# Three gaps of 16 bytes in the rows that the matmuls read

## The chip, the cores and the metric

One NeuronCore of a Trainium2 chip runs the whole program. The metric is the device time of one execution in microseconds (us); the kernel before took 2957.85 us in the median of three runs (2950.77, 2957.85 and 2959.75). TensorE (PE) multiplies, and its weight loads are shown apart as PEld. VectorE is DVE, ScalarE is ACT, GpSimd is POOL and SyncE is SP.

## The reference, cut to what matters

The reference is a two-layer decoder trunk for 256 tokens of width 2048, all in float32. Layer 0 mixes with a gated DeltaNet, layer 1 with differential attention; each is followed by an MLP and a gated embedding:

```python
h = h + gated_deltanet(rmsnorm(h, norm_mix[0]), ...)      # layer 0
h = h + diff_attention(rmsnorm(h, norm_mix[1]), k, v, ...)  # layer 1
hn = rmsnorm(h, norm_mlp[i])
h = h + jnp.square(jax.nn.relu(hn @ mlp_w1[i])) @ mlp_w2[i]   # 2048 -> 8192 -> 2048
gate = jax.nn.sigmoid(rmsnorm(h, norm_ple[i]) @ ple_w_gate[i])
h = h + (p[i] @ ple_w_proj[i]) * gate
```

After layer 0 the stream is normalised once more and projected to the keys and values of layer 1. Nearly all arithmetic is the product of 256 rows with a large weight matrix.

## The kernel before, in words

Every large product is made of two halves of each operand: a value is rounded to fp32r (the "hi" half), the rest is the "lo" half, and three matmuls (hi·hi, hi·lo, lo·hi) are summed in PSUM. `chunk` (lines 118 to 134) brings 1 MB of weights with one DMA from SP's queue into `raw`, ACT rounds it 1024 columns at a time into `whi` (line 131), and DVE subtracts into `wlo` (line 132). Three buffers each let this run ahead of PE.

Two loops use the pieces. They differ in what stands still in the array:

- `g2` (lines 137 to 153) makes a transposed product. A 128x128 block of weights is the stationary operand, and the 256 columns of one k tile of x are the moving one. For each k tile and each block of 128 output columns there is a triple: line 150 (`xh` past `whi`), line 151 (`xl` past `whi`), line 152 (`xh` past `wlo`). It is used for the gates, keys, queries and values of the DeltaNet, for the first half of the MLP, and for queries and keys of the attention: 3600 triples, 10,800 matmuls of 256 columns.
- `g1` (lines 155 to 169) makes a plain product. A 128x128 block of x is stationary, and 512 columns of weights move, in triples of lines 166, 167 and 168. It is used for z of the DeltaNet, V of the attention, and every output product.

In the MLP, `first(q)` is a block of 256 triples of `g2` (768 matmuls) and `second(q)` one of `g1`; they run in the order first 0, first 1, second 0, first 2, second 1, first 3, second 2, second 3.

`xpair` (lines 200 to 203) allots one tile `xh` and one `xl` with room for 16 k tiles of 256 floats and 128 floats more, and hands out two views of each: one that begins `SHIFT` = 112 floats (448 bytes) into the tile, and one that begins at 0. Each k tile is a row of 256 floats (1024 bytes), and row follows row without a gap. The shifted view (`self.xa`, and `xb` in the attention) is the moving operand of all of `g2`; it is also the stationary operand of `g1` for z and V (384 triples). The view at 0 (`self.xs`, `oT`) is stationary only. `transposed` (lines 185 to 198) fills a view row by row: ACT writes the hi half (line 197) and DVE the lo half (line 198).

As built, the tiles `xh` and `xl` and all `raw`, `whi` and `wlo` tiles begin at multiples of 512 bytes within a partition, the hidden halves `hidh` and `hidl` (and `ph`, `pl`) 256 bytes past one, and `oh` and `ol` 384 bytes past one. So in `g2` every moving row begins 448 bytes past a multiple of 512 and every stationary block at a multiple of 512.

The float32 operands of lines 389 and 666 begin at a multiple of 512 and 32 bytes past one.

The order of the work is that of the program on each engine; PE takes its matmuls in that order.

Of the kernel before, what the change touches and what calls it, by code (L numbers as in the profile page):

```python
# [18 lines left out]
T = 256  # L19
NT = T // P  # L20
KD = D // P
# [11 lines left out]
SHIFT = 112  # L33
LAM_INIT = 0.8 - 0.6 * math.exp(-0.3 * 1)
POST = 1.0 - LAM_INIT


class Trunk:
    def __init__(self, ctx, tc, d, out):
        self.ctx, self.tc, self.nc, self.d, self.out = ctx, tc, tc.nc, d, out  # L40
        pool = lambda name, bufs, **kw: ctx.enter_context(tc.tile_pool(name=name, bufs=bufs, **kw))
        self.const = pool("const", 1)
        self.wraw = pool("wraw", 3)
        self.whl = pool("whl", 3)
        self.main = pool("main", 1)
        self.small = pool("small", 2)
        self.acc = pool("acc", 4, space=bass.MemoryType.PSUM)
        self.mis = pool("mis", 4, space=bass.MemoryType.PSUM)
        self.dram = pool("dscr", 1, space=bass.MemoryType.DRAM)
# [6 lines left out]
    def constants(self):  # L56
# [3 lines left out]
        nc.vector.memset(self.eps[:, 1:2], EPS * HD)  # L60
        nc.vector.memset(self.eps[:, 2:3], EPS / POST ** 2)
        nc.scalar.activation(self.eps[:, 3:4], self.eps[:, 0:1], AF.Sqrt)
# [137 lines left out]
    def xpair(self, pool, which):  # L200

        tiles = [pool.tile([P, KD * T + 128], F32R, name=n + which) for n in ("xh", "xl")]
        return tuple(tuple(t[:, o:o + KD * T].rearrange("p (k t) -> p k t", k=KD) for t in tiles) for o in (SHIFT, 0))

    def rowcast(self, r, dst):

# [416 lines left out]
    def attention(self, h):  # L623
        nc, tc, d = self.nc, self.tc, self.d
        with ExitStack() as c:
# [60 lines left out]
            def values(hd, aT):  # L686
# [7 lines left out]
                for t in range(NT):  # L694
                    nc.scalar.activation(o[:, t * T:(t + 1) * T], po[:, t * T:(t + 1) * T], AF.Square, accum_out=ss[:, t:t + 1])
                nc.scalar.activation(ss, ss, AF.Sqrt, scale=1.0 / (2 * HD * POST ** 2), bias=self.eps[:, 2:3])
                nc.vector.reciprocal(ss, ss)
# [95 lines left out]
```

## Time and profile before

| what | value |
|---|---|
| median of three runs | 2957.85 us |
| profiled execution | 2951.79 us, of which the span from first to last instruction is 2950.0 us |
| mean granted TensorE clock | 0.996 |
| PE busy | 2909.7 us (99% of the span), 18730 matmul records |
| DVE busy | 1782.8 us (60%) |
| ACT busy | 1451.8 us (49%) |
| DMA | 527.19 MB, mean 179 GB/s |

Matmuls overlap in the records: a matmul of 256 columns is shown with 0.28 us, while the next starts 0.11 or 0.12 us after it. So pace is read from start to start, or from how many matmuls a stretch of time holds (a count takes in those that had begun before the stretch, so one matmul's length is added to the stretch).

### The profile page before, as it was taken

What the parts mean: (1) busy time and instruction counts of PE and PEld (TensorE: products, weight loads), DVE (VectorE), ACT (ScalarE), POOL (GpSimd) and SP (SyncE); (2) the same over time, 40 slices, a digit from 0 to 9 for tenths busy, and PEclk for the clock granted to TensorE, in tenths of its full rate; (3) what the DMA queues carried; (4) which work ended last, traced back from release to release, by engine and by line L of the source; (5) the groups of instructions that cost most, each with busy time, mean ns of one, the idle gap of its engine ahead of it and who ended that gap; (6) DMA issues with size and microseconds to landing.
All of it is one profiled execution on the core that took longest, in us unless ns stands there. A gap on an engine that the chain in (4) does not pass through costs nothing.

```text
span 2950.0 us, 44777 instructions
## 1 busy us (share of the span) xinstructions
PE 2909.7 (99%) x18730; PEld 2626.2 (89%) x18730; DVE 1782.8 (60%) x2324; ACT 1451.8 (49%) x1947; POOL 60.4 (2%) x64
## 2 busy tenths in 40 slices
PE   8999999999999999999999999999999999999998
PEld 8989889988988998989988889987899899898886
DVE  7879766666666555555555565567555555555565
ACT  5655555545545443444434553367544444344454
POOL 1011000000000000000000000000000000000000
PEclk9999999999999999999999999999999999999999
DMA  6654544455445665655565556654566565556654
GB/s 200 207 168 140 175 161 138 149 175 161 133 143 182 194 196 190 188 194 189 186 198 189 178 170 198 191 166 144 183 192 197 189 192 192 188 186 198 202 172 155
DMA packets 289595, 527.19 MB, mean 179 GB/s; under 512 B 25966, under 2 KB 44560, under 8 KB 289264
## 3 DMA queue, kind: packets, MB, share of 16 engines
q1 hardware_dynamic: 288160, 521.77, 55.3%
q8 instruction: 147, 2.41, 0.3%
q0 software_dynamic: 816, 2.03, 0.2%
q10 hardware_dynamic: 416, 0.53, 0.1%
q14 instruction: 56, 0.46, 0.0%
HBM read 520.03 MB, written 4.26 MB: 178 GB/s over the span
## 4 chain that ended last, share of the span: by engine, by line
PE 93%; DVE 4%; ACT 2%; DMA 0%; issue 0%; POOL 0%; ACTq 0%; DVEq 0%
PE accb L166 16%; PE accb L167 16%; PE accb L168 16%; PE accb L151 13%; PE accb L152 13%; PE accb L150 13%; PE misb L429 2%; DVE wlo L132 1%; ACT whi L131 1%; PE misb L434 1%; PE misb L412 0%; PE misb L444 0%; PE misb L193 0%; PE misb L421 0%; DMA h<-x 0%
## 5 line engine op out<-in xcount | busy, mean ns | idle before, releaser
L132 DVE TENSOR_TENSOR wlo<-raw,whi 128x1024 fp32r<-128x1024 f32 x970 | 1190.1, 1228 | 985.0 <-ACT whi L131 983.6
L131 ACT CAST whi<-raw 128x1024 fp32r<-128x1024 f32 x970 | 1019.2, 1051 | 1296.8 <-PE accb L168 677.5
L150 PE MATMUL accb<-xha,whi 128*128 128x256 f32 x3344 | 939.4, 281 | 0.8 <-ACT whi L131 0.8
L151 PE MATMUL accb<-xla,whi 128*128 128x256 f32 x3344 | 937.6, 280 | 1.6 <-DVE xla L198 1.6
L152 PE MATMUL accb<-xha,wlo 128*128 128x256 f32 x3344 | 936.9, 280 | 0.5 <-DVE wlo L132 0.5
L152 PEld LDWEIGHTS accb<-xha,wlo 128*128 128x128 f32 x3344 | 633.2, 189 | 0.7 <-DVE wlo L132 0.7
L151 PEld LDWEIGHTS accb<-xla,whi 128*128 128x128 f32 x3344 | 629.7, 188 | 2.4 <-DVE xla L198 2.2
L150 PEld LDWEIGHTS accb<-xha,whi 128*128 128x128 f32 x3344 | 630.4, 189 | 1.4 <-ACT whi L131 1.0
L168 PE MATMUL accb<-whi,hidl 128*128 128x512 f32 x1024 | 398.5, 389 | 0.0
L167 PE MATMUL accb<-wlo,hidh 128*128 128x512 f32 x1024 | 398.5, 389 | 0.0
L166 PE MATMUL accb<-whi,hidh 128*128 128x512 f32 x1024 | 398.5, 389 | 0.0
L166 PE MATMUL accb<-whi,xha 128*128 128x512 f32 x640 | 254.2, 398 | 1.2 <-ACT xha L197 1.2
L167 PE MATMUL accb<-wlo,xha 128*128 128x512 f32 x640 | 252.8, 395 | 0.1
L168 PE MATMUL accb<-whi,xla 128*128 128x512 f32 x640 | 251.9, 394 | 0.0
L168 PEld LDWEIGHTS accb<-whi,hidl 128*128 128x128 f32 x1024 | 192.3, 188 | 40.1
L166 PEld LDWEIGHTS accb<-whi,hidh 128*128 128x128 f32 x1024 | 192.3, 188 | 39.9
L167 PEld LDWEIGHTS accb<-wlo,hidh 128*128 128x128 f32 x1024 | 192.3, 188 | 39.1
L166 PEld LDWEIGHTS accb<-whi,xha 128*128 128x128 f32 x640 | 120.4, 188 | 26.2 <-ACT xha L197 2.5
L167 PEld LDWEIGHTS accb<-wlo,xha 128*128 128x128 f32 x640 | 120.5, 188 | 25.0 <-DVE wlo L132 1.4
L168 PEld LDWEIGHTS accb<-whi,xla 128*128 128x128 f32 x640 | 120.3, 188 | 24.2
L166 PE MATMUL accb<-whi,oh 128*128 128x512 f32 x256 | 101.1, 395 | 0.8 <-ACT oh L469 0.8
L167 PE MATMUL accb<-wlo,oh 128*128 128x512 f32 x256 | 101.1, 395 | 0.0
(276 smaller groups left out, 2616.5 us busy)
## 6 DMA issues: line engine op xcount, KB each, us to landing
raw<-mlp_w SPq DMA_DIRECT2D x256, 1024.0 KB, 5.2
raw<-gdn_w_in SPq DMA_DIRECT2D x97, 1024.0 KB, 5.1
raw<-gdn_w_out SPq DMA_DIRECT2D x32, 1024.0 KB, 5.0
raw<-ple_w_gate SPq DMA_DIRECT2D x32, 1024.0 KB, 5.0
raw<-w_kv SPq DMA_DIRECT2D x32, 1024.0 KB, 5.2
raw<-diff_w_q SPq DMA_DIRECT2D x16, 1024.0 KB, 5.0
raw<-diff_w_o SPq DMA_DIRECT2D x16, 1024.0 KB, 5.0
gcb<-gcd SPq DMA_DIRECT2D x16, 256.0 KB, 4.3
```

Source lines behind the costliest of these rows:

```text
L131: nc.scalar.copy(hi, sl)
L132: nc.vector.tensor_tensor(lo, sl, hi.bitcast(F32), ALU.subtract)
L150: nc.tensor.matmul(o, hi[:, k, cs], xh[:, kt], start=kt == 0 and ct % 2 == 0, stop=False, skip_group_check=True)
L151: nc.tensor.matmul(o, hi[:, k, cs], xl[:, kt], start=False, stop=False, skip_group_check=True)
L152: nc.tensor.matmul(o, lo[:, k, cs], xh[:, kt], start=False, stop=kt == nk - 1, skip_group_check=True)
L166: nc.tensor.matmul(banks[t], xh[:, kt, ts], hi[:, k], start=kt == 0, stop=False)
L167: nc.tensor.matmul(banks[t], xh[:, kt, ts], lo[:, k], start=False, stop=False)
L168: nc.tensor.matmul(banks[t], xl[:, kt, ts], hi[:, k], start=False, stop=kt == nk - 1)
L429: nc.tensor.matmul(ps[:, h * P:(h + 1) * P], NTt[:, 2 * h + c], X[:, h * P:(h + 1) * P], start=True, stop=True)
L434: nc.tensor.matmul(ps[:, h * P:(h + 1) * P], UB[:, 2 * h + c], X[:, h * P:(h + 1) * P], start=True, stop=True)
```

## The change

The shifted view is no longer one block of 16 rows. A small class holds four blocks of four rows, and each block begins 4 floats (16 bytes) later than it would have, counted from the one before. Rows 0 to 3 stay where they were, 448 bytes into the tile; rows 4 to 7 lie 16 bytes later than before, rows 8 to 11 lie 32 bytes later, rows 12 to 15 lie 48 bytes later. The room of 128 floats at the tile's end holds it: no tile changes its size or place. The view at 0 is as it was.

```diff
+class Rows:
+    def __init__(self, tile, first):
+        n = KD // 4 * T
+        self.parts = [tile[:, first + g * (n + 4):first + g * (n + 4) + n].rearrange("p (k t) -> p k t", t=T) for g in range(4)]
+
+    def __getitem__(self, at):
+        k = at[1]
+        return self.parts[k // (KD // 4)][(at[0], k % (KD // 4)) + tuple(at[2:])]
...
     def xpair(self, pool, which):
         tiles = [pool.tile([P, KD * T + 128], F32R, name=n + which) for n in ("xh", "xl")]
-        return tuple(tuple(t[:, o:o + KD * T].rearrange("p (k t) -> p k t", k=KD) for t in tiles) for o in (SHIFT, 0))
+        return tuple(Rows(t, SHIFT) for t in tiles), tuple(t[:, :KD * T].rearrange("p (k t) -> p k t", k=KD) for t in tiles)
```

No instruction is added, removed or moved on any engine, and each waits for what it waited for. What differs are start addresses: of one operand of 8964 matmuls (8100 moving rows in `g2`, 864 stationary blocks in `g1`), of the output of 60 writes by ACT, and of the output and one input of 60 by DVE.

## Rows read from the trace of the kernel before

**Rows 1.** The page: busy time, PE clock by slices, the chain.
```profile
PE 2909.7 (99%) x18730; PEld 2626.2 (89%) x18730; DVE 1782.8 (60%) x2324; ACT 1451.8 (49%) x1947; POOL 60.4 (2%) x64
...
PEclk9999999999999999999999999999999999999999
...
PE 93%; DVE 4%; ACT 2%; DMA 0%; issue 0%; POOL 0%; ACTq 0%; DVEq 0%
```

**Rows 2.** Waits of PE, longest first: us in total, times, longest.
```profile
PE misb L193 <- DVE w_mix L76: 3.4, 1, 3.4
...
PE accb L152 <- DVE wlo L132: 1.8, 3, 0.7
PE accb L150 <- ACT xhb L197: 1.6, 2, 1.2
```

**Rows 3.** Busy time by windows of `g2`: us, busy (xcount), clock, DMA, GB/s.
```profile
56.00:76.00 20.00, 20.00 (x172) 20.00 (x171) 14.44 (x20) 10.97 (x12) 0.00 (x0) 1.00 0.69 227
28.00:51.00 23.00, 23.00 (x198) 23.00 (x197) 18.78 (x30) 12.73 (x15) 0.00 (x0) 1.00 0.56 182
91.00:159.00 68.00, 68.00 (x579) 68.00 (x579) 55.50 (x98) 37.70 (x50) 0.00 (x0) 1.00 0.67 205
932.00:1102.00 170.00, 170.00 (x1503) 170.00 (x1502) 96.10 (x99) 81.73 (x95) 0.00 (x0) 1.00 0.61 192
1190.00:1279.00 89.00, 89.00 (x758) 89.00 (x757) 46.82 (x46) 39.90 (x44) 0.00 (x0) 1.00 0.60 190
1759.00:1919.00 160.00, 160.00 (x1414) 160.00 (x1413) 80.95 (x75) 62.24 (x59) 0.00 (x0) 1.00 0.62 197
2134.00:2303.00 169.00, 169.00 (x1494) 169.00 (x1493) 95.09 (x98) 81.33 (x95) 0.00 (x0) 1.00 0.62 193
```

**Rows 4.** Instructions in order of time on PE, MLP of layer 0: start, us.
```profile
1189.69 0.39 PE L168 MATMUL accb<-whi,hidl 128*128 128x512 f32 x1
1189.92 0.28 PE L150 MATMUL accb<-xha,whi 128*128 128x256 f32 x1
1190.04 0.28 PE L151 MATMUL accb<-xla,whi 128*128 128x256 f32 x1
1190.15 0.28 PE L152 MATMUL accb<-xha,wlo 128*128 128x256 f32 x1
1190.27 0.28 PE L150 MATMUL accb<-xha,whi 128*128 128x256 f32 x1
```

**Rows 5.** Weight loads by group, 1368 to 1457 us: xcount | busy us, mean ns.
```profile
L152 PEld LDWEIGHTS accb<-xha,wlo 128*128 128x128 f32 x253 | 48.6, 192 | 0.0
L150 PEld LDWEIGHTS accb<-xha,whi 128*128 128x128 f32 x252 | 47.3, 188 | 0.0
```

**Rows 6.** Line 168 of `g1`: duration ns min/median/max, first and last start us.
```profile
L168 PE MATMUL accb<-whi,hidl x1024: 388/389/394, 1103.3 to 2833.3; 128*128 128x512 f32 x171
L168 PE MATMUL accb<-whi,ol x256: 390/393/404, 323.3 to 923.9; 128*128 128x512 f32 x128
L168 PE MATMUL accb<-whi,xlb x128: 387/389/485, 2032.5 to 2125.4; 128*128 128x512 f32 x128
```

**Rows 7.** Matmuls by group in V of the attention, 1926 to 1940 us.
```profile
L168 PE MATMUL accb<-whi,xla 128*128 128x512 f32 x21 | 8.3, 394 | 0.0
L167 PE MATMUL accb<-wlo,xha 128*128 128x512 f32 x21 | 8.2, 392 | 0.0
L166 PE MATMUL accb<-whi,xha 128*128 128x512 f32 x21 | 8.2, 388 | 0.0
```

**Rows 8.** Two float32 matmuls of 256 columns: duration ns min/median/max.
```profile
L389 PE MATMUL misb<-kT x32: 377/379/382, 187.5 to 859.1; 128*128 128x256 f32 x32
L666 PE MATMUL misb<-kT,qT x32: 379/381/383, 1942.7 to 2045.9; 128*128 128x256 f32 x32
```

**Rows 9.** Line 197, ACT's writes of the hi halves: duration ns min/median/max.
```profile
L197 ACT ACTIVATE xha<-misb,cols x80: 454/480/540, 925.2 to 2845.3; 128x256 fp32r<-128x256 f32 x80
L197 ACT ACTIVATE xha<-misb,w_mix x16: 465/473/488, 17.2 to 26.8; 128x256 fp32r<-128x256 f32 x16
```

## The prediction

> **What bounds the kernel now.** I read the page first. PE is busy for 99% of the span, the chain that ended last runs over PE for 93%, and the granted clock stands at full speed in every slice, so it is at the 2.4 GHz level throughout [rows 1]. The waits of PE come next: the longest entry is 3.4 us in total, and the one for weights just 1.8 us [rows 2]. So nothing feeds PE too late. The kernel lasts as long as PE's matmuls take one after another, and only their pace matters.
>
> A clock that stands still should mean one pace for equal matmuls. The windows say otherwise [rows 3]. In the first two MLP blocks of layer 0 (932 to 1102 us), 1503 matmuls of 256 columns fit into 170.28 us (the window and one matmul's 0.28): 113.3 ns each. In the attention (1759 to 1919) it is 160.28/1414 = 113.4, in layer 1's first two blocks 169.28/1494 = 113.3. But in the third block of layer 0 it is 89.28/758 = 117.8 ns, and in the DeltaNet's first stages 117.7, 117.6 and 117.9 (20.28/172, 23.28/198, 68.28/579). The third and fourth block of both layers, four in all, read like the row 1190:1279. Nothing waits there either: PE is busy in the whole window, the clock is the same, DMA share and GB/s are alike. I call these the fast and the slow pace; they differ by 4.5 ns.
>
> Two more things matter about them. The slow pace is there from the first matmul: the first one after a `g1` block at 1189.92, the next starts 0.12, 0.11, 0.12 us later [rows 4]. And it holds for a whole block of 768, as the fast one holds for two blocks. In the slow pace every third weight load is longer, 192 ns beside 188 [rows 5]. So the slow pace is something between the moving row's stream and the weight load that runs beside it, and once the two run at a given offset in time they keep it.
>
> Does the address decide? In `g1` the same 512 moving columns run past stationary blocks at different addresses. Past the hidden tile (256 bytes past a multiple of 512) and past the attention's `xlb` at 0 a record lasts 389 ns, past `ol` at 384 it lasts 393 [rows 6]. Past `xa` at 448, in V, the three lines last 388, 392 and 394, which is 7 ns a triple more than three times 389 [rows 7]. Taken as distance from stationary to moving start, modulo 256 bytes: 0 costs nothing, 128 about 4 ns a matmul, 192 about 2.3. In `g2` the distance is 64 (stationary at 0, moving at 448), and costs 0 or 4.5. So addresses do count, and 0 is a clean distance in `g1`.
>
> **The change, part by part.** *Instructions.* None is added or moved, so no wait, queue or DMA changes by itself. The 60 writes of ACT and 60 of DVE go to starts 16, 32 or 48 bytes later. Line 197 took 480 ns in the median for one group and 473 for another of the same shape [rows 9]; if the new starts cost that difference either way, it is 60 x 7 ns = 0.4 us. I take 0.
>
> *Moving rows of `g2`.* Three quarters of 10,800 matmuls, 8100, read from a new phase. Named stretches at the slow pace are four MLP blocks of 768 (3072) and 172 + 198 + 579 in the early DeltaNet, 4021 in all: 4021 x 4.5 ns = 18.1 us is what the slow pace costs today. Named stretches at the fast pace are four MLP blocks (3072) and the attention's 1536: 4608. The remaining 2171 are cut into short groups by the DeltaNet's small matmuls; I leave them out.
>
> The new distances are 48, 32 and 16 for the second, third and fourth quarter. No row has such a distance. The nearest are 64 (0 or 4.5 ns) and 0 (nothing, in `g1`). Read as a straight line between them, the slow share of the moved quarters falls to three quarters, a half and a quarter of today's, a half on average: 18.1 x 0.75 x 0.5 = 6.8 us gained. That reading treats each matmul by itself. The other takes into account that a pace holds: 16 k tiles come round for every 512 output columns, the last quarter at distance 16, and the first quarter of the next round follows it without a pause. If a stream that has become fast at 16 or 32 stays fast when it comes back to 64, only the first quarters after each restart stay slow, and nearly all is gained; I put it at 0.85 of 18.1 = 15.4 us. I take the middle of the two, 11 us. The ends of this term are a gain of 18.1 (all fast) and a loss of 4608 x 4.5 = 20.7 us (all that is fast becomes slow), without a cost that belongs to the phase alone, below.
>
> *Stationary blocks of `g1`.* 384 triples of `xa` at 7 ns are 2.7 us. Their distance goes from 192 to 208, 224 and 240, towards the clean 256. By the same straight line three quarters of them lose half: 2.7 x 0.75 x 0.5 = 1.0 us gained. Ends: 2.7 gained, or, at the 4 ns a matmul of distance 128, 864 x (4 - 2.3) = 1.5 us lost.
>
> *Cover.* A faster PE needs its weights sooner. In the fast windows DMA moves 192 to 197 GB/s at a share of 0.61 to 0.62 and PE stays busy throughout [rows 3], so the slow blocks can be fed at the fast pace too. In the DeltaNet's short groups part of a gain may turn into waiting for DVE; those groups are not in the sum.
>
> *Sum.* Against the profiled execution's own 2951.8 us (span 2950.0, 1.8 around it): 2951.8 - 11 - 1 = 2939.8. The median of the runs shown is 6 us higher, which is about what 1350 more matmuls at the slow pace would make, so executions may differ in which stretches are slow. I add half of it: 2943 us.
>
> **A rule against this.** Between one stationary address and another, line 168's record goes from 389 to 394 ns at one clock [rows 6, 7]. The Trainium skill, "TensorE: Matmul & The Clock Gate", section "Step-by-step: what each phase is for", says that PE reads the moving operand and the weights through two independent ports, so that loading the next weights takes no read bandwidth from the running matmul. By that rule the start address is of no account and the change makes 0 us. Rows 6 and 7 speak against it in its plain form; the same outcome is rival 1.
>
> **Rivals.**
> 1. *Start addresses do nothing here, or what is gained in one stretch is lost in another.* For it: both paces exist at one and the same distance of 64, so the address alone doesn't decide. Against it: `g1`'s four distances [rows 6, 7]. By itself 0 us, by the straight line alone 8 us gained; with the 3 us for the median that is 2947 to 2955, and the runs shown scatter up to 2960.
> 2. *The new phases hold the slow pace.* The place is the MLP's fast blocks and the attention. The rows would be no better at 16 to 48 than at 64, and a stream kicked at each quarter would fall into the slow pace and stay. Price: 4608 x 4.5 = 20.7 us, or 15.6 if only the moved three quarters are slow. It decides the sign when more than about half of the fast matmuls turn. From 2951.8 and the 3 us for the median that gives 2970 to 2976, with the short groups up to 2982. For it: the third MLP block is slow from its first matmul, though the `g1` block ahead of it ran without a pause [rows 4], so the slow pace is easily entered.
> 3. *A row that doesn't start on a 64-byte boundary touches 17 pieces of 64 bytes instead of 16.* The fast pace of 113.3 ns is 272 cycles of 2.4 GHz for 256 columns, 17 for each 16 columns, and 16 columns are 64 bytes. If every piece touched costs 17 cycles, however little of it is used, a moved row costs 289 cycles, 7.1 ns more: 8100 x 7.1 = 57 us, about 3005. If it costs one cycle for the boundary alone, 0.42 ns, it is 3.4 us. Against it: the float32 matmuls whose operands start 32 bytes past a multiple of 64 (line 666) last 381 ns, those at 0 (line 389) last 379 [rows 8]; 2 ns on 8100 rows would be 16 us. But these stream more slowly, so they bound it loosely.
>
> **How the numbers follow.** The forecast (the slow pace goes in good part, 2926 to 2949) has 0.45. Rival 1 has 0.24, rival 2 has 0.17, rival 3 in its large form 0.10, and 0.04 is left for anything else on either side. A measurement of this kernel can tell about 0.3%, here 9 us, so faster begins below 2949. Faster: 0.45 and a little of rival 1, 0.47. Slower: rivals 2 and 3 and a little of rival 1 and the rest, 0.31. The same: 0.22. The likeliest case gives 2943, its own range is 2926 to 2949. The range that should hold 8 in 10 goes from 2926, which leaves the two slow terms all gone with a little of the DeltaNet's short groups, up to 2982, the top of rival 2; rival 3 is left outside.
>
> **What would show it.** In the windows after the change, the third and fourth MLP blocks should hold about 788 matmuls in 89 us instead of 758, and weight loads of 192 ns should become rare. If the pace changes every four k tiles (48 matmuls), the address acts on each matmul by itself; if a block is of one pace throughout, the lock in time rules. V's three lines should come nearer to 389. The prediction is wrong if the blocks that were fast read 117.8 or more, if a third pace near 120 ns appears in the moved quarters (rival 3), or if the counts in all windows stand as they were.

## The result, and the profile after

The changed kernel took 2971.74 us in the median of five runs (2969.56 to 2975.82), the kernel before 2956.84 (2950.77 to 2959.75). The ratio is 1.0063, with an interval of 1.005 to 1.0077: 0.6% slower, where 0.5% faster was forecast. Ratios here and below are the recorded ones, which compare the runs of the two kernels and needn't be the quotient of the two medians (here 1.005). One execution of the last run below, 3203.12 us at a granted clock of 0.849, is left out of its ratio.

The page shows the same machine with nothing new to wait for. The first line is the busy time of each engine, the second the granted clock by slices, the others the longest wait of PE and that for weights:

```profile
PE 2929.8 (99%) x18730; PEld 2645.0 (89%) x18730; DVE 1783.2 (60%) x2324; ACT 1452.6 (49%) x1947; POOL 58.1 (2%) x64
...
PEclk9999999999999999999999999999999999999999
...
PE misb L205 <- DVE w_mix L88: 4.2, 1, 4.2
...
PE accb L164 <- DVE wlo L144: 1.6, 3, 0.7
```

PE has the same 18730 matmuls as in [rows 1], is busy 20.1 us longer, and the span grew by 20.8 us, from 2950.0 to 2970.8. The longest wait of PE grew by 0.8 us, the one for weights is 0.2 shorter [rows 2]. So the time went into the pace of the matmuls themselves. The windows of [rows 3], read in the changed kernel (us, busy and count of PE, PEld, DVE, ACT, POOL, then clock, DMA share, GB/s):

```profile
932.00:1102.00 170.00, 170.00 (x1453) 169.98 (x1452) 94.73 (x101) 81.46 (x98) 0.00 (x0) 1.00 0.58 181
1190.00:1279.00 89.00, 89.00 (x725) 87.48 (x724) 47.40 (x47) 40.02 (x44) 0.00 (x0) 1.00 0.60 188
28.00:51.00 23.00, 23.00 (x197) 23.00 (x197) 18.88 (x30) 12.30 (x15) 0.00 (x0) 1.00 0.53 172
91.00:159.00 68.00, 68.00 (x582) 68.00 (x582) 54.99 (x96) 38.31 (x50) 0.00 (x0) 1.00 0.67 207
```

The first two MLP blocks hold 1453 matmuls where they held 1503: 170.28/1453 = 117.2 ns instead of 113.3. The stretches that ran at 117.8 hardly differ: 117.3 instead of 117.9 from 91 to 159 us, 118.2 instead of 117.6 from 28 to 51, and 117.2 from 1215 to 1265 (below; the window from 1190 now begins in `g1`, whose matmuls are longer). So not one pace took over from the other; there are new ones. One round of 16 k tiles in layer 1's MLP shows them. The rows are the first matmul of each quarter of four k tiles, and of the next round (start, us):

```profile
2190.57 0.28 PE L162 MATMUL accb<-xha,whi 128*128 128x256 f32 x1
...
2196.04 0.28 PE L162 MATMUL accb<-xha,whi 128*128 128x256 f32 x1
...
2201.76 0.28 PE L162 MATMUL accb<-xha,whi 128*128 128x256 f32 x1
...
2207.44 0.28 PE L162 MATMUL accb<-xha,whi 128*128 128x256 f32 x1
...
2213.07 0.28 PE L162 MATMUL accb<-xha,whi 128*128 128x256 f32 x1
```

A quarter is 48 matmuls. It takes 5.47, 5.72, 5.68 and 5.63 us: 114.0 ns a matmul in the quarter that stayed at distance 64 (stationary start minus moving start, modulo 256 bytes), 119.2 at distance 48, 118.3 at 32, and 117.3 at 16. Over the whole program, from start to start, the means are 114.7, 119.1, 118.3 and 117.3, and every block of the MLP and the attention has the last three to 0.1 ns.

The sum closes. I add up the times from one matmul's start to the next within `g2`, and take off 113.33 ns each (226.67 in `g1`). Times over 150 ns (300 in `g1`), mostly at restarts and waits, stay out. What is left over was 22.8 us in `g2` and 7.5 in `g1`; now it is 41.7 and 9.4. That is 18.9 and 1.9 us more, 20.8 together, the whole growth of the span; with the long times it is 21.4, so what else changed is under 1 us. By quarters, `g2`'s 41.7 are 3.4 (distance 64), 14.8, 13.1 and 10.4; the 22.8 before were 6.1, 5.8, 5.6 and 5.3.

V of the attention answers to [rows 7] (xcount | busy us, mean ns):

```profile
L179 PE MATMUL accb<-wlo,xha 128*128 128x512 f32 x21 | 8.3, 394 | 0.0
L180 PE MATMUL accb<-whi,xla 128*128 128x512 f32 x21 | 8.2, 393 | 0.0
L178 PE MATMUL accb<-whi,xha 128*128 128x512 f32 x20 | 7.9, 394 | 0.0
```

The three lines last 394, 393 and 394 ns, a sum of 1181 where it was 1174: V did not come nearer to 389, it moved away. From start to start, z and V went from 229.2 and 229.3 ns a matmul to 230.5 and 231.0.

### The profile page after: what moved, and what is told of

Its sections match the earlier page's. It is cut to its first block, busy times and chain, and to the rows that moved or that the text cites. A ratio compares the mean times of both kernels' runs of the same rounds, so it can differ in the third digit from the quotient of the medians.

```text
span 2970.8 us, 44777 instructions
## 1 busy us (share of the span) xinstructions
PE 2929.8 (99%) x18730; PEld 2645.0 (89%) x18730; DVE 1783.2 (60%) x2324; ACT 1452.6 (49%) x1947; POOL 58.1 (2%) x64
## 4 chain that ended last, share of the span: by engine, by line
PE 95%; DVE 3%; ACT 1%; DMA 1%; issue 0%; POOL 0%; ACTq 0%; SPq 0%; DVEq 0%
PE accb L179 16%; PE accb L178 16%; PE accb L180 16%; PE accb L163 14%; PE accb L164 13%; PE accb L162 13%; PE misb L441 2%; DVE wlo L144 1%; PE misb L446 1%; PE misb L424 0%; ACT whi L143 0%; PE misb L456 0%; PE misb L205 0%; PE misb L433 0%; DMA raw<-gdn_w_in 0%
```

## The experiments

The pace of the kernel before in the two windows that the runs below are read in, one at either of its paces:

```profile
960.00:1080.00 120.00, 120.00 (x1061) 120.00 (x1061) 66.80 (x65) 56.86 (x64) 0.00 (x0) 1.00 0.62 194
1215.00:1265.00 50.00, 50.00 (x427) 50.00 (x426) 27.94 (x29) 23.63 (x27) 0.00 (x0) 1.00 0.59 184
```

That is 120.28/1061 = 113.4 ns and 50.28/427 = 117.8 ns. In the changed kernel:

```profile
960.00:1080.00 120.00, 120.00 (x1025) 120.00 (x1025) 65.00 (x63) 55.55 (x63) 0.00 (x0) 1.00 0.60 187
1215.00:1265.00 50.00, 50.00 (x429) 50.00 (x428) 26.41 (x27) 23.18 (x26) 0.00 (x0) 1.00 0.60 190
```

117.3 and 117.2 ns. My theory after the result was that a start off a multiple of 64 bytes costs; the question was whether it is the moving row's own start or its difference from the weights'. The runs whose edit shows `self.parts` start from the changed kernel, and so do the two scans; the others start from the kernel before.

**Is 0 a clean distance?**

```diff
-SHIFT = 112
+SHIFT = 0
```

> The shifted view begins at 0 bytes instead of 448, without gaps, so that moving row and weight block both begin at multiples of 512 bytes in g2. Theory A (what costs is the difference of moving row and weight block within 64 bytes, here 0): g2 stays at its two paces of 113.3 and 117.8 ns, no 119, and z and V lose their 7 ns a triple; total 2930 to 2957 us. Theory B (the moving row's own start within 64 bytes costs, whatever the weights do; here 0): the same. Theory C (the distance modulo 256 bytes sets a sliding price: 64 gave 113.3, 48 gave 119.1, 32 gave 118.3, 16 gave 117.3, so 0 should give about 116): all of g2 near 116 ns, no block at 113.3; about 2957 us.

```profile
960.00:1080.00 120.00, 120.00 (x1002) 120.00 (x1001) 64.48 (x63) 54.22 (x63) 0.00 (x0) 1.00 0.58 182
1215.00:1265.00 50.00, 50.00 (x419) 50.00 (x418) 26.02 (x26) 22.34 (x26) 0.00 (x0) 1.00 0.58 183
```

2993.27 us, ratio 1.0146 (1.0131 to 1.0161). Every block of the MLP and the attention runs at 120.0 ns, the slowest pace of all the longer stretches, with both operands at multiples of 512 bytes. Theories A and B, which put the price on bytes within 64, had 2957 at most and fall as they stood; so does C's straight line, which had 116. In `g1` the same distance is good: z and V came down from 229.2 and 229.3 to 227.8 and 228.6 ns. What is clean in `g1` is the worst in `g2`.

**One phase alone, without jumps.**

```diff
-SHIFT = 112
+SHIFT = 120
```

> No gaps; all rows of the shifted view begin 480 instead of 448 bytes into the tile, 32 bytes past a multiple of 64, while the weights stay where they are. All three theories: every g2 block runs at the 118.3 ns that the third quarter showed, none at 113.3. 10,800 matmuls x (118.3 - 115.5, the mean before) = 30 us more: about 2987 us. Had the loss come from the jumps between phases and not from the phases, g2 would stay at 113.3 and 117.8 and the time near 2957.

```profile
960.00:1080.00 120.00, 120.00 (x1017) 120.00 (x1016) 64.86 (x64) 55.98 (x64) 0.00 (x0) 1.00 0.59 187
1215.00:1265.00 50.00, 50.00 (x425) 50.00 (x424) 27.08 (x26) 22.38 (x26) 0.00 (x0) 1.00 0.60 189
```

2982.76 us, ratio 1.011 (1.0095 to 1.0125). 118.3 ns in both windows, as the third quarter of the changed kernel. So the distance itself costs, and not the jumps between distances.

**Own start or difference?**

```diff
+        self.pad = pool("pad", 1)
+        self.pad.tile([P, 8], F32, name="pad")
         self.whl = pool("whl", 3)
```

> The kernel before with 32 bytes of padding ahead of all weight buffers and activations, so that moving rows and weight blocks alike begin 32 bytes past a multiple of 64, at the same differences as before. Theory A and C (differences count): g2 at 113.3 and 117.8 ns, g1 past the hidden tile at 226.7, about 2957 us. Theory B (a row's own start counts): g2 at 118.3 throughout as with the weights left in place, +30 us, and g1's moving weights slower too; 2985 us or more.

```profile
960.00:1080.00 120.00, 120.00 (x1061) 120.00 (x1061) 66.43 (x64) 57.13 (x65) 0.00 (x0) 1.00 0.62 195
1215.00:1265.00 50.00, 50.00 (x426) 50.00 (x426) 28.34 (x29) 23.73 (x28) 0.00 (x0) 1.00 0.59 187
```

2956.84 us, ratio 1.0027 (1.0014 to 1.0041). The moving rows start 32 bytes past a multiple of 64 as in the run just told, but the weight blocks do too, and in both windows the paces are those of the kernel before, to one matmul in the count. So at these starts it is the difference of the two that sets the pace, and not the row's own start; no other pair of starts with one difference was tried, but for the last run below. That the total is 0.3% up I can't place: the profiled execution's span was 2951.9 us, and the ten runs scatter from 2951.34 to 2970.68. Which of the two paces a stretch has can change even so. In the first block of keys, the kernel before and this run:

```profile
30.00:49.00 19.00, 19.00 (x164) 19.00 (x163) 15.34 (x24) 10.95 (x14) 0.00 (x0) 1.00 0.57 180
30.00:49.00 19.00, 19.00 (x170) 19.00 (x169) 15.45 (x24) 11.20 (x13) 0.00 (x0) 1.00 0.58 180
```

That is 19.28/164 = 117.6 ns and 19.28/170 = 113.4, at the same distance of 64.

**Multiples of 64.**

```diff
-SHIFT = 112
+SHIFT = 80
...
-        self.parts = [tile[:, first + g * (n + 4):first + g * (n + 4) + n].rearrange(...) for g in range(4)]
+        self.parts = [tile[:, first + g * (n + 16):first + g * (n + 16) + n].rearrange(...) for g in range(4)]
```

> The three gaps are 64 bytes instead of 16, and the first row begins 320 bytes into the tile, so that the four quarters lie at distances 192, 128, 64 and 0 modulo 256 bytes from the weights, each at a multiple of 64. Theories A and B: no quarter at 117.3, 118.3 or 119.1 for its phase; all at 113.3 or the held 117.8; 2930 to 2960 us. Theory C: the pace changes by quarter, worst at distance 128; near or over 2970 us.

2974.44 us, ratio 1.0085 (1.0068 to 1.0102). From start to start in the MLP: 117.9 ns at distance 192, 118.7 at 128, 114.2 at 64 and 119.6 at 0. The pace changes by quarter, as C had it, though the worst distance is 0 and not 128, and the 64-byte grid gives no protection.

**Only one k tile moved.**

```diff
-        self.parts = [...]
+        self.rows = [tile[:, first + k * T + 12 * (k == KD - 1):][:, :T] for k in range(KD)]
...
+        return self.rows[at[1]][(at[0],) + tuple(at[2:])]
```

> Only the last of the 16 k tiles is moved, by 48 bytes (distance 16); the other fifteen keep distance 64. Theory L (at distance 64 both paces are possible, and a stream that comes in from another distance falls into the fast one): all blocks run at 113.3 ns in k tiles 0 to 14, with a few longer matmuls on the way back in; 675 matmuls at 117.3 cost 2.7 us, the ways back in about 7 us, and the 23 us that g2 now spends over 113.3 ns a matmul go: about 12 us less than before, 2936 to 2945. Theory M (the pace of a block is set where it starts, by what ran ahead of it): the third and fourth MLP blocks stay at 117.8, and the time is 2 to 8 us above the kernel before.

The windows are four rounds of 16 k tiles that follow each other in the first MLP:

```profile
953.00:972.00 19.00, 19.00 (x164) 19.00 (x163) 9.60 (x11) 7.92 (x9) 0.00 (x0) 1.00 0.62 204
975.00:993.00 18.00, 18.00 (x161) 18.00 (x160) 10.06 (x10) 7.83 (x10) 0.00 (x0) 1.00 0.64 203
997.00:1016.00 19.00, 19.00 (x164) 19.00 (x163) 9.90 (x10) 8.10 (x10) 0.00 (x0) 1.00 0.64 204
1020.00:1038.00 18.00, 18.00 (x161) 18.00 (x160) 9.51 (x10) 7.83 (x9) 0.00 (x0) 1.00 0.64 206
```

2956.32 us, ratio 1.0008 (0.9999 to 1.0016): no difference, and neither theory as stated. The rounds take turns: 19.28/164 = 117.6 ns, 18.28/161 = 113.5, 117.6, 113.5. Twelve matmuls at distance 16 turn a stream at 113.3 into one at 117.8 and the other way about. Distance 64 does hold two paces; how the stream comes in picks one.

**Two scans.** In the first, k tile k begins 16 x k bytes late from 0 on, in the second 4 x k bytes late from 448 on:

```diff
-SHIFT = 112
+SHIFT = 0    # scan by 16 bytes alone
...
+        self.rows = [tile[:, first + k * T + 4 * k:][:, :T] for k in range(KD)]   # scan by 16 bytes
+        self.rows = [tile[:, first + k * T + k:][:, :T] for k in range(KD)]       # scan by 4 bytes, SHIFT = 112
```

> k tile k begins 16 x k bytes late, from 0 on, so that the 16 k tiles lie at the distances 0, 240, 224, ... 16 modulo 256 bytes. Theory D (the distance modulo 256 sets the price): the known points come back within 0.7 ns, 120.0 at 0, 117.3 at 16, 118.3 at 32, 119.2 at 48, 117.9 at 192, 118.7 at 128, and 64 is at or near 113.3; nothing is known of the others. Theory J (jumps between k tiles cost by themselves): every k tile is above its known point, by 2 ns or more.

> k tile k begins 4 x k bytes late, from 448 bytes on, so that the distances are 64, 60, 56, ... 4. If the price belongs to a moving row that starts off a 64-byte boundary with respect to the weights, it jumps to 119 ns or more at the first step, 60. If it slides with the distance, it climbs by about 1.5 ns a step from 113.3 at 64 to 119.2 at 48, and falls again to 117.3 at 16.

One run each: 2974.96 and 2987.56 us. Worked out from the starts in the MLP, distance and mean ns, in the order in which the k tiles run:

```
by 16:  0 119.1  240 119.2  224 116.3  208 118.4  192 113.6  176 119.2  160 120.0  144 113.3
      128 117.8  112 119.0   96 117.3   80 118.9   64 114.8   48 118.8   32 118.5   16 117.2
by 4:  64 117.8   60 120.7   56 119.8   52 117.6   48 117.0   44 120.7   40 121.0   36 117.1
       32 118.1   28 119.9   24 121.0   20 116.0   16 117.5   12 121.8    8 119.4    4 116.9
```

There is no straight line anywhere. The first step of 4 bytes, from 64 to 60, already goes from 117.8 to 120.7, and then the pace rises and falls about every 16 bytes. Theory D gets 16 and 32 (within 0.2 ns), and 48 in the scan by 16; it misses 0 and 128 by 0.9, 64 by 1.5 and 192 by 4.3 ns. Theory J is refuted, since no known point lies 2 ns above. The paces repeat from round to round, but some depend on the neighbour ahead: 192 is 113.6 here and 117.9 above, 48 is 117.0 to 119.1. Twelve matmuls a k tile can be too few for a pace to settle. Only 144 stood at 113.3 throughout the MLP.

**The two good points of the scan, by themselves.**

```diff
-SHIFT = 112
+SHIFT = 28    # 112 bytes, distance 144
+SHIFT = 16    # 64 bytes, distance 192 (a run of its own)
```

> No gaps; all rows of the shifted view begin 112 bytes into the tile (distance 144 modulo 256, 48 bytes past a multiple of 64), the one point of the scan where every k tile of the MLP ran at 113.3 ns. Theory D (the distance sets the pace, and 144 has the fast pace alone): g2 at 113.3 in all blocks, 22 us of its surplus gone; z and V at a distance of 112, whose price in g1 is unknown, between 0 and 8 ns a matmul, or 9 us more and 8 us less than before: 2922 to 2942 us. Theory P (the pace at a distance depends on where the stream comes from; 144 was fast only because it was entered from 160): some blocks at 113.3, others at 117 or more, 2940 to 2985 us.

> No gaps; all rows begin 64 bytes into the tile (distance 192). In the four quarters 64 bytes apart this distance ran at 117.9 ns, entered from the end of a block at distance 0; in the scan by 16 bytes it ran at 113.6, entered from 208. Theory P (two paces at one distance, set by how the stream comes in and then held): blocks at 113.6 and blocks at 117.9, or all at one of them; 2935 to 2975 us. Theory D: one pace only, between them.

At 112 bytes:

```profile
960.00:1080.00 120.00, 120.00 (x1061) 120.00 (x1061) 66.75 (x65) 56.92 (x64) 0.00 (x0) 1.00 0.62 195
1215.00:1265.00 50.00, 50.00 (x444) 50.00 (x443) 29.86 (x30) 24.49 (x29) 0.00 (x0) 1.00 0.62 195
```

At 64 bytes:

```profile
960.00:1080.00 120.00, 120.00 (x1021) 120.00 (x1021) 65.40 (x65) 55.85 (x64) 0.00 (x0) 1.00 0.59 187
1215.00:1265.00 50.00, 50.00 (x427) 50.00 (x426) 26.55 (x26) 22.78 (x26) 0.00 (x0) 1.00 0.59 187
```

Distance 144 took 2940.11 us, ratio 0.9948 (0.9936 to 0.9961): faster than both kernels. All MLP blocks stand at 113.3 to 113.5 ns on average, 50.28/444 = 113.2 where it was 117.8. In the MLP and the attention the stream finds that pace by itself within one to nine k tiles of a restart, as theory D had it. In the DeltaNet's short groups, which other matmuls break up, it often doesn't: their queries and values average 115.8 and 115.6 ns. `g2`'s surplus fell from 22.8 to 5.4 us, of which 4.4 are in those groups; `g1` paid 12.2 - 7.5 = 4.7 back, 4.0 of it with z and V, at 233.2 and 233.4 ns a matmul.

Distance 192 took 2976.87, ratio 1.0066 (1.0052 to 1.0079), with 117.8 ns in all of the MLP and the attention. But its first block of keys ran at 19.28/170 = 113.4 ns:

```profile
30.00:49.00 19.00, 19.00 (x170) 19.00 (x170) 14.96 (x23) 11.69 (x14) 0.00 (x0) 1.00 0.54 170
```

So 192 holds two paces, as 64 does and as theory P had it, and the 113.6 of the scan was a matter of entry, that is of how the stream comes in.

**Is it modulo 256?**

```diff
-SHIFT = 112
+SHIFT = 92    # 368 bytes
```

> No gaps; all rows begin 368 bytes into the tile, 256 bytes later than in the run at 112 bytes. If the distance counts modulo 256 (144 again), this is that run once more: g2 at 113.3 to 113.6 ns in the MLP and the attention, 2938 to 2943 us, 0.5% less than the kernel before. If it counts over more than 256 bytes, the pace is another, 116 ns or more, and the time 2950 us or above.

```profile
960.00:1080.00 120.00, 120.00 (x1061) 120.00 (x1061) 66.77 (x65) 56.91 (x64) 0.00 (x0) 1.00 0.62 195
1215.00:1265.00 50.00, 50.00 (x444) 50.00 (x443) 29.86 (x30) 24.62 (x29) 0.00 (x0) 1.00 0.62 194
```

2942.67 us, ratio 0.996 (0.9932 to 0.9988), and the counts of the run at 112 bytes. For this distance, 256 bytes more change nothing.

## Why the prediction was wrong

*What bounds the kernel* was right: pace of PE alone, at one clock, two paces 4.5 ns apart, decided by addresses and held over time. Writes, waits, queues and DMA made less than 1 us of difference, as said. Two slips bear on no number of the forecast: 20.28/172 is 117.9 and not 117.7 ns, and 57 us on 2951.8 are 3009 and not 3005.

*The step that failed* is the price of the three new distances. It was read "as a straight line" between 64 and 0, with 0 taken as clean because it costs nothing in `g1`. Both halves were wrong. In `g2` distance 0 is the slowest of all the longer stretches, 120.0 ns, so a row of `g1` is no end of the range for `g2`. And between two points the price doesn't slide: in the scan by 4 bytes it goes from 117.8 to 120.7 ns in one step and from 121.0 to 116.0 in another. In place of a gain of 6.8 to 15.4 us stands: the three moved quarters went from 16.7 us of surplus to 38.3, a loss of 21.6; the quarter left alone gained 2.7, from 6.1 to 3.4. The pace changes every four k tiles, which the prediction had named as the sign that the address acts; only the price at each address was wrong.

*That a stream comes back fast* was right for this change: the first quarter runs at 113.9 to 114.9 ns in the blocks of the MLP and the attention, and where a block begins at the held 117.8, that is broken from its second round on. But it is worth 2.7 us, since only a quarter of the matmuls are there to gain. And it is luck of the entry: with a single moved tile the rounds alternate.

*z and V*, all that the change touches in `g1`, were to gain 1.0 us and lost 1.4; the rest of the 1.9 that `g1` lost is in products that the change doesn't touch. The ends taken for them were 2.7 gained and 1.5 lost, so the size lies just inside; the sign was wrong, by the same straight line.

*Rival 2* had the sign, the size (15.6 to 20.7, measured 18.9 in `g2`) and the time. Its mechanism was close: the moved quarters are slow, but at paces of their own (119.1, 118.3, 117.3), not at the held 117.8, and the unmoved one doesn't fall into it. That the measured time lies within 2926 to 2982 is owed to this rival alone, which had a chance of 0.17. *Rival 3* is refuted: rows 32 bytes past a multiple of 64 (everything moved) and 48 bytes past (distance 144) run at 113.3, so its price isn't what moved the quarters. *Rival 1* had 0 us and is refuted by the quarters.

The rule behind rival 1 is that PE's two ports keep the weight load from taking read bandwidth from the running matmul (the Trainium skill, "TensorE: Matmul & The Clock Gate", section "Step-by-step: what each phase is for"). As far as the pace goes, the runs speak against it: 113.3 to 120.0 ns with another start of the moving rows alone. Whether it is read bandwidth that the two take from each other, no run here shows.

Shown is that the start of the moving rows sets the pace, together with how the stream comes in, and, at the pair of starts tried, that the difference from the weights' start counts. What in the chip makes it so stays open, and so does why 144 is good, and 0 is bad here and good in `g1`.

## What to carry to other kernels

When equal matmuls show two paces at one clock without a wait, compare the start addresses of the two operands, and scan the distance: one kernel with a different offset for each k tile gives 16 points in one run. Then run a candidate alone, since a short stretch can show a pace that it only brought along, and read it in every stage, since one distance can hold two paces. Don't carry a good distance from one shape of matmul to another, and don't interpolate between two of them.

## What the runs showed of the hardware that was not expected

- The pace of 256-column fp32r matmuls, with a weight load each, went from 113.3 to 120.0 ns (6%) in longer stretches with nothing but the moving rows' start address changed.
- At distance 64 both 113.3 and 117.8 ns are stable for hundreds of matmuls, and twelve matmuls at another distance turn one into the other, both ways. Distance 192 shows the same two paces, 113.4 in the first block of keys and 117.8 in the MLP.
- A start at a multiple of 512 bytes for both operands was the slowest arrangement that `g2` ran in longer stretches (120.0 ns); moving rows that start 112 or 368 bytes past a multiple of 512 were the fastest (113.3 ns).
